# Keys ordered by token mod 8, fixed PSUM tiles and a spread inverse in a two-layer hybrid encoder

## The chip, the core and the metric

The kernel runs on one core of one Trainium2 chip. The core has five engines that work side by side, each from a queue of its own in order: TensorE (PE in the profile, with its weight loads as PEld), VectorE (DVE), ScalarE (ACT), GpSimd (POOL) and SyncE (SP), which here issues the DMA transfers. Data lives in HBM, in the on-chip SBUF (128 partitions) and in PSUM, into which TensorE writes its products. The metric is the time of one execution on the device in microseconds; shorter is better.

## The reference

One sequence of 1024 tokens of width 1024, float32, goes through two layers. Each layer has a token mixer and a squared-ReLU MLP, both between RMS norms.

```python
# layer 0, mixer A (8 heads of 64): three branches, merged by softmax-denominator weights
for window, dil in ((128, 1), (512, 4), (2048, 16)):
    radius = window // 2 // dil                     # 64 keys on each side in every branch
    split = lambda t: t.reshape(nB, H, S // dil, dil, hd).transpose(0, 1, 3, 2, 4)
    o, lse = banded_attention(split(q), split(k), split(v), bias, radius, radius)
o = sum(softmax(lse over branches) * o)             # and mixer B: banded GQA with a sink
# layer 1, mixer: one scan per direction, 16 heads of 64
sa = einsum('bhvk,bhk->bhv', state, -kk_t)
state = state * w_t + sa * (kk_t * a_t) + v_t * k_t
out_t = einsum('bhvk,bhk->bhv', state, r_t)
```

The attention's scores get a relative-position bias. With 1024 tokens, the third branch (dilation 16) is computed here in classes of tokens mod 8, with a bias that masks every second key.

## The kernel before

**Stages in order of time.** The v projection and bias tables (to 100 us), dilated attention A (100 to 455), banded attention B (to 547), the output projection (to 675), the MLP of layer 0 (to 1380), the projections of layer 1 (to about 1953), the chunked recurrence (its loop runs from 2077 to 2860), the output projection of layer 1 and its MLP. The change touches attention A (with the helpers that B also uses) and the recurrence.

**Who orders the work.** The program is written in order, and a planner then simulates it and lays down each engine's queue: among the instructions that are ready in its simulated time, the one that was written earliest goes first. Instructions inside the recurrence's units are written under `tc.high_priority(50)` (L1374), so they go ahead of other work. DMA issues stand in SP's queue, and a transfer that waits there holds up those behind it. Two engines that touch the same tile wait for each other by semaphores.

**Attention A.** Four pairs of heads, one after the other (L618). For each pair, v is loaded from DRAM in three layouts, one per branch: `v1` (11 blocks of 128 tokens in natural order, 3 loads), `v2` (classes mod 4, 2 loads) and `v3` (classes mod 8, 1 load). `make_q` (L536) and `make_k` (L548) project the pair's heads by PE in halves of 512 tokens and copy the results out of PSUM by ACT and DVE in turn: q as one tile whose two row halves hold a high and a low part, k as two tiles, high and low. The tokens stand in natural order in both. For each head and branch, `banded` (L566) goes through 8 tiles of 128 queries: two score products (L575, L576), the sum with the bias and the row minimum by DVE (L578), the exponential by ACT (L583), one or two transposes by PE (L587), a copy by ACT (L588), and one or two products with v (L592). Branch 1 reads the queries and 256 keys as runs. Branch 2 picks its 128 queries and 256 keys by a step of 4 tokens, branch 3 its 128 queries and 128 keys by a step of 8, both with

```python
def every(x, r, n, step):
    return x[:, r:r + (n - 1) * step + 1:step]
```

The bias of a head and branch is loaded from a table in DRAM (L645 to L648). `normalise` (L597) divides four tiles at a time. At the end of the pair the outputs of branches 2 and 3 (o2, o3) go to DRAM and come back in natural order as n2, n3 (L656 to L663); DVE and POOL merge them with o1 (L665 to L687).

**The recurrence.** Tokens go in chunks of 64; a step G handles two chunks of both directions and four heads, four steps are a batch, and eight batches make the 16 heads. Per step, `scan` (L1367) handles 8 units: 2 chunks x 2 head pairs x 2 directions, so four chains (`ci`) run interleaved, each with its own PSUM tile `ch` (tag c0 to c3, allocated anew for every unit) and its state `h`. A unit is: the state scaled by ACT (L1384); sums of two products (L1386, L1390), whose two halves stand in the same 64 columns on different rows; their copy to `y`, one half by ACT (L1392) and one by DVE (L1393); a product with the inverse (L1395), copied to `sv` by DVE and ACT (L1397, L1398); the new state's sum (L1401), which DVE scales and adds in two operations of 64x64 (L1407 for a first unit, L1410); the output products (L1416, L1421), written to the same columns as the state's sum; and their copy by ACT (L1424). After each unit `side()` (L1531) writes a piece of other work: `prep` of a step that lies eight ahead, `post` of the next step, `finish` of the last one.

`invert` (L1286) makes the inverses for a whole batch: two loads (L1290), 30 rounds of two DVE operations on all heads (L1295, L1297), then stores and loads through DRAM (L1302 to L1315). It is written as one piece at the second step of the batch before (L1513 to L1517); what follows it, up to the first half of the loads, is stepped by `first` (L1481) through `side()`, behind `post` of the next step. `post` of the next batch's first step, written at the fourth step, reads its results.

Of the kernel before, what the change touches and what calls it, by code (L numbers as in the profile page):

```python
# [15 lines left out]
P = 128  # L16
# [9 lines left out]
def fsl(i, n):  # L26
    return slice(i * n, (i + 1) * n)
# [444 lines left out]
def attention(tc, g, ap, ocd):  # L472
    nc = tc.nc
    with ExitStack() as es:
# [73 lines left out]
        def make_k(widx):  # L548
# [3 lines left out]
            for half, ps in project(widx):  # L552
                hs = fsl(half, 512)
                for j in range(2):
                    a, b = fsl(j, HD), fsl(1 - j, HD)
                    nc.scalar.activation(ks[j][a, hs], ps[a], AF.Copy)
                    nc.vector.tensor_tensor(out=kl[j][a, hs], in0=ps[a], in1=ks[j][a, hs], op=ALU.subtract)
                    nc.scalar.activation(ks[j][b, hs], ps[a], AF.Copy)
                    nc.vector.tensor_tensor(out=kl[j][b, hs], in0=ps[a], in1=ks[j][a, hs], op=ALU.subtract)
# [6 lines left out]
        def banded(tiles, q, k, bias, vtile, vcols, mneg, sink=None, W=256):  # L566
# [3 lines left out]
            for i, (qsl, ksl, blocks, boff) in enumerate(tiles):  # L570
# [4 lines left out]
                nc.tensor.matmul(ps[:, :n], lhsT=every(q, *qsl), rhs=every(kh, *ksl), start=True, stop=False)  # L575
                nc.tensor.matmul(ps[:, :n], lhsT=every(q, *qsl), rhs=every(kl, *ksl), start=False, stop=True)  # L576
# [32 lines left out]
        t1 = []  # L609
        for tt in range(TT):  # L610
            k0 = min(max(0, P * tt - 64), T - 256)
            bl = (7, 8) if tt == 0 else (9, 10) if tt == TT - 1 else (tt - 1, tt)
            t1.append(((P * tt, P, 1), (k0, 256, 1), bl, k0 - P * tt + P))
        t2 = [((512 * hf + r, P, 4), (r, 256, 4), (2 * r, 2 * r + 1), P * (1 - hf)) for hf in range(2) for r in range(4)]

        t3 = [((r, P, 8), (r, P, 8), (r,), 0) for r in range(8)]

        for pr in range(4):  # L618
            v1 = vp.tile([P, 11, 130], F32, tag="v1", name="v1")
            v2 = vp.tile([P, 8, 130], F32, tag="v2", name="v2")  # L620
            v3 = vp.tile([P, 8, 130], F32, tag="v3", name="v3")
            vc = vd[:, fsl(pr, P)]
            for v in (v1, v2, v3):
# [3 lines left out]
            blocks = lambda x: x.rearrange("(i p) c -> p i c", p=P)  # L627
            nc.sync.dma_start(out=v1[:, 0:7, cc], in_=blocks(vc[64:960, :]))
            nc.sync.dma_start(out=v1[:, 7:9, cc], in_=blocks(vc[0:256, :]))
            nc.sync.dma_start(out=v1[:, 9:11, cc], in_=blocks(vc[768:1024, :]))  # L630
            v4 = vc.rearrange("(j r) c -> j r c", r=4)
# [181 lines left out]
RC = 64  # L813
# [885 lines left out]
```

## Time and profile before

| | |
|---|---|
| median of 3 runs | 3665.36 us (3656.43 to 3675.8) |
| the profiled execution | 3664.62 us, its span 3662.9 us |
| granted PE clock over the span | 0.91 of full speed |
| attention A (100 to 455 us) | PE 339, DVE 184, ACT 198, POOL 26 us busy |
| the recurrence's loop (2077 to 2860 us) | PE 620, DVE 603, ACT 467, POOL 288 us busy, clock 0.80 |

A row of a group of instructions reads: line, engine, operation, output <- inputs, shapes, count | busy us, mean ns of one | idle time of its engine before them, and what ended it. A row of a stretch reads: its bounds and length, the busy time of each engine with the number of instructions, the granted clock of PE, the DMA engines' share and GB/s. A row of the waits reads: who waited <- for whom: us in total, times, the longest. A row of the timeline reads: start, length, engine, line, operation.

### The profile page before, as it was taken

The numbers are of one execution on the slowest core, as the hardware profiler recorded it, in microseconds if no ns is written. First come the engines' busy times: TensorE is split into PE (matmuls) and PEld (weight loads), VectorE is DVE, ScalarE is ACT, GpSimd is POOL, SyncE is SP. The second block draws the span as 40 slices with busy tenths as digits, with TensorE's granted clock in tenths as the row PEclk, the third lists the DMA queues.
The fourth block names the chain that finished last, engine by engine and source line by source line (L and its number), as shares of the span: only waits on it lengthen the run. The fifth ranks groups of instructions, "written<-read, shape, count | busy, mean of one in ns | idle before, by whom it ended". The sixth has DMA issues, their size and how long they took to land. (4 is left out here: it accounts for less than half of the span.)

```text
span 3662.9 us, 61199 instructions
## 1 busy us (share of the span) xinstructions
PE 3175.4 (87%) x22168; PEld 2587.1 (71%) x22168; DVE 2529.6 (69%) x4649; ACT 1849.7 (50%) x4244; POOL 1768.2 (48%) x1610
## 2 busy tenths in 40 slices
PE   7999998899999888888887687788777889999988
PEld 6788887688777676665566566666665768877766
DVE  3355564744499978977855778887776474449996
ACT  2366564455543347754433365555666445554333
POOL 1000001465598884455566344444431156558887
PEclk9999998899999998999896687778887899999999
DMA  6222214232231133257765354445444423323113
GB/s 202 72 80 81 72 55 171 76 138 108 70 139 37 79 113 107 95 185 232 228 221 155 94 127 107 106 127 122 121 100 133 129 84 135 115 71 131 42 74 115
DMA packets 408204, 425.70 MB, mean 116 GB/s; under 512 B 138155, under 2 KB 321579, under 8 KB 401756
## 3 DMA queue, kind: packets, MB, share of 16 engines
q1 hardware_dynamic: 406716, 417.58, 36.3%
q0 software_dynamic: 1184, 4.20, 0.4%
q8 instruction: 174, 2.85, 0.3%
q14 instruction: 130, 1.06, 0.1%
HBM read 290.83 MB, written 138.20 MB: 117 GB/s over the span
## 5 line engine op out<-in xcount | busy, mean ns | idle before, releaser
L101 PE MATMUL pm<-bhi,lo 128*128 128x512 f32 x840 | 331.8, 398 | 49.5 <-DVE lo L130 49.3
L130 DVE TENSOR_TENSOR lo<-x,hi 128x512 fp32r<-128x512 f32 x300 | 323.3, 1084 | 62.4 <-ACT hi L129 62.0
L129 ACT ACTIVATE hi<-x 128x512 fp32r<-128x512 f32 x300 | 189.1, 631 | 334.1 <-PE pm L100 129.1
L100 PE MATMUL pm<-blo,hi 128*128 128x512 f32 x840 | 330.2, 393 | 7.7 <-POOL blo L130 7.3
L99 PE MATMUL pm<-bhi,hi 128*128 128x512 f32 x840 | 319.2, 393 | 7.1 <-ACT bhi L129 6.7
L127 POOL TENSOR_TENSOR x<-w1r 128x512 f32<-128x512 f32 x160 | 214.6, 1345 | 203.1 <-DVE lo L130 178.3
L130 POOL TENSOR_TENSOR blo<-bx,bhi 128x512 fp32r<-128x512 f32 x138 | 221.1, 1603 | 30.5 <-ACT bhi L129 29.7
L1268 POOL TENSOR_TENSOR af<-af,amask 128x512 f32<-128x512 f32 x128 | 164.8, 1293 | 147.2 <-ACT af L1267 109.3
L101 PEld LDWEIGHTS pm<-bhi,lo 128*128 128x128 f32 x840 | 157.6, 188 | 101.9 <-DVE lo L130 70.8
L1264 PE MATMUL A<-zr,bk 128*128 128x128 f32 x1024 | 189.5, 349 | 44.3 <-DVE bk L1257 38.2
L905 POOL TENSOR_TENSOR wl<-wr,wh 128x512 fp32r<-128x512 f32 (+2 forms) x144 | 162.0, 1136 | 126.3 <-ACT wh L904 94.8
L127 POOL TENSOR_TENSOR bx<-w 128x512 f32<-128x512 f32 x140 | 215.1, 1539 | 9.5
L1264 PEld LDWEIGHTS A<-zr,bk 128*128 128x128 f32 x1024 | 168.1, 252 | 57.2 <-POOL bk L1258 22.0
L127 DVE TENSOR_TENSOR x<-h 128x512 f32<-128x512 f32 x140 | 195.6, 1409 | 5.3 <-ACT h L268 2.7
L100 PEld LDWEIGHTS pm<-blo,hi 128*128 128x128 f32 x840 | 158.4, 189 | 47.7 <-POOL blo L130 14.5
L99 PEld LDWEIGHTS pm<-bhi,hi 128*128 128x128 f32 x840 | 158.4, 189 | 40.0 <-ACT bhi L129 7.6
L99 PE MATMUL mm<-xmh,wh 128*128 128x512 f32 x384 | 163.0, 443 | 10.1 <-ACT wh L904 4.7
L1416 PE MATMUL c<-af,sv 128*64 128x64 f32 x1024 | 96.8, 273 | 74.7 <-DVE h L1410 67.7
L1410 DVE SCALAR_TENSOR_TENSOR h<-c,pc,hd 64x64 f32<-64x64 f32 x448 | 127.0, 284 | 49.6 <-PE c L1401 28.7
L583 ACT ACTIVATE S<-S,mneg 128x256 f32<-128x256 f32 (+2 forms) x256 | 124.7, 499 | 69.1 <-DVE mneg L578 46.2
L335 DVE TENSOR_TENSOR acc<-acc,pm 128x512 f32<-128x512 f32 x256 | 158.1, 675 | 0.3 <-PE pm L101 0.3
L886 DVE SCALAR_TENSOR_TENSOR x<-u,mu,x 128x512 f32<-128x512 f32 x192 | 153.4, 832 | 7.0 <-ACT x L884 4.3
(369 smaller groups left out, 9933.0 us busy)
## 6 DMA issues: line engine op xcount, KB each, us to landing
w1r<-in_mlp_w_dram SPq DMA_DIRECT2D x32, 1024.0 KB, 5.5
w<-in_mlp_w_dram SPq DMA_DIRECT2D x32, 1024.0 KB, 6.7
x<-x SPq DMA_DIRECT2D x64, 386.0 KB, 3.3
hd<-h SPq DMA_DIRECT2D x24, 1024.0 KB, 4.2
h<-hd SPq DMA_DIRECT2D x24, 1024.0 KB, 8.2
wr<-in_w_rkv_dram SPq DMA_DIRECT2D x96, 256.0 KB, 2.8
x<-xo SPq DMA_DIRECT2D x32, 512.0 KB, 3.7
rk<-rk SPq DMA_DIRECT2D x64, 256.0 KB, 3.7
```

The source lines that it names most:

```text
L99: nc.tensor.matmul(out, lhsT=ahi, rhs=bhi, start=start, stop=False)
L100: nc.tensor.matmul(out, lhsT=ahi, rhs=blo, start=False, stop=False)
L101: nc.tensor.matmul(out, lhsT=alo, rhs=bhi, start=False, stop=stop)
L127: add.tensor_tensor(out=y, in0=x, in1=blocks[term[2]], op=ALU.add if term[1] == "+" else ALU.subtract)
L129: nc.scalar.activation(hi, x, AF.Copy)
L130: sub.tensor_tensor(out=lo, in0=x, in1=hi, op=ALU.subtract)
L335: dve.tensor_tensor(out=a, in0=a, in1=banks[j], op=ALU.add if sign == "+" else ALU.subtract)
L886: nc.vector.scalar_tensor_tensor(out=x, in0=at(2 * i), scalar=mu[:, i, c, kt:kt + 1], in1=x, op0=ALU.mult, op1=ALU.add)
L905: nc.gpsimd.tensor_tensor(out=wlo, in0=wr, in1=whi, op=ALU.subtract)
L1264: nc.tensor.matmul(ps[:, fsl(u, P)], lhsT=bk[:, u, j].rearrange("p a b -> p (a b)"), rhs=zr[:, u].rearrange("p a b -> p (a b)"), start=Tru ...
L1268: nc.gpsimd.tensor_tensor(out=o, in0=o, in1=consts["amask"].unsqueeze(1).to_broadcast([P, 4, P]), op=ALU.mult)
L1410: nc.vector.scalar_tensor_tensor(out=hn[rows, cols], in0=ch[rows, 128:192], scalar=pc[rows, u:u + 1], in1=hd[rows, cols], op0=ALU.mult, op ...
```

## The change

**Attention.** `make_k` can write k in an order by token mod 8 (class r, then a = token // 8), by writing with a step of 128 elements. q is projected as before, and POOL copies it to `q8` in the same order. The key part of a tile is now a function of the k tile: branch 1 takes 8 runs of 32 keys, branch 2 two runs of 128, branch 3 one run of 128; queries of branches 2 and 3 are runs of `q8`. A tile of branch 2 now has the queries of one class mod 8 in place of 128 consecutive ones mod 4. `v1` becomes 16 blocks, two per query tile in the order of the keys, with 16 loads; `v2` is gone and branch 2 uses `v3`. The biases of branches 1 and 2 are loaded in natural order and put in the order of the keys by POOL (3 and 2 copies a head). n2 and n3 use the buffers of o2 and o3.

**The recurrence.** The four PSUM tiles are allocated once and set to zero. The two halves of the first sum stand in columns of their own, so that the tile's first 128 columns hold a block matrix with zeros elsewhere; one ACT copy of 128x128 makes `y`, and DVE's copy is gone. The state's sum has columns 256 to 383 in the same way, and one DVE operation of 128x128 makes the new state.

**The inverse.** It is begun at the batch's first unit (the loads), continued by two rounds (of two DVE operations) after each of units 4 to 18, and what follows, up to the first half of the loads, is written after unit 20 of 32.

```diff
+        def make_k(widx, perm=False):
...
+                kh_, kl_ = ([x.rearrange("p (r a) -> p a r", r=8)[:, fsl(half, 64)] if perm else x[:, fsl(half, 512)]
+                             for x in y] for y in (ks, kl))
+                if perm:
+                    ps = runs(ps, 8)
                 for j in range(2):
                     a, b = fsl(j, HD), fsl(1 - j, HD)
-                    nc.scalar.activation(ks[j][a, hs], ps[a], AF.Copy)
+                    nc.scalar.activation(kh_[j][a], ps[a], AF.Copy)
...
-                nc.tensor.matmul(ps[:, :n], lhsT=every(q, *qsl), rhs=every(kh, *ksl), start=True, stop=False)
+                nc.tensor.matmul(ps[:, :n], lhsT=every(q, *qsl), rhs=ksl(kh), start=True, stop=False)
...
-        t2 = [((512 * hf + r, P, 4), (r, 256, 4), (2 * r, 2 * r + 1), P * (1 - hf)) for hf in range(2) for r in range(4)]
-        t3 = [((r, P, 8), (r, P, 8), (r,), 0) for r in range(8)]
+        by8 = lambda x: x.rearrange("p (r a) -> p r a", r=8)
+        k0s = [min(max(0, P * tt - 64), T - 256) for tt in range(TT)]
+        t1 = [((P * tt, P, 1), lambda x, a=k0 // 8: by8(x)[:, :, a:a + 32], (2 * tt, 2 * tt + 1), 256 * (0 if tt == 0 else 2 if tt == TT - 1 else 1))
+              for tt, k0 in enumerate(k0s)]
+        t2 = [((r * P, P, 1), lambda x, r=r % 4: by8(x)[:, r:r + 5:4], (r % 4, r % 4 + 4), 256 * (r // 4)) for r in range(8)]
+        t3 = [((r * P, P, 1), lambda x, r=r: x[:, fsl(r, P)], (r,), 0) for r in range(8)]
...
+            for tt, k0 in enumerate(k0s):
+                win = vc[k0:k0 + 256, :].rearrange("(a i r) c -> i r a c", i=2, r=4)
+                for i in range(2):
+                    nc.sync.dma_start(out=v1[:, 2 * tt + i, cc], in_=win[i])
...
+            q8 = [qp.tile([P, T], F32R, tag=f"qp{j}", name=f"qp{j}", bufs=1) for j in range(2)]
+                    nc.gpsimd.tensor_copy(q8[j].rearrange("p (r a) -> p a r", r=8)[:, fsl(hf, 64)], runs(qs[j][:, fsl(hf, 512)], 8))
...
+                for i, f in enumerate((128, 64, 0)):
+                    nc.gpsimd.tensor_copy(b1[:, fsl(i, 256)].rearrange("p (r a) -> p r a", r=8), runs(nat[:, f:f + 256], 8).transpose([0, 2, 1]))
...
+                for i, f in enumerate((1, 0)):
+                    nc.gpsimd.tensor_copy(b2[:, fsl(i, 256)].rearrange("p (r a) -> p r a", r=2), runs(nat[:, f:f + 256], 2).transpose([0, 2, 1]))
...
-            n2 = op.tile([P, TT, 130], F32, tag="n2", name="n2")
+            n2 = op.tile([P, TT, 130], F32, tag="o2", name="n2")
...
+        chs = [psC.tile([P, 512], F32, name=f"c{d}") for d in range(4)]
+        for x in chs:
+            nc.vector.memset(x, 0.0)
...
-                            ch = psC.tile([P, 512], F32, tag=f"c{ci}", name=f"c{ci}")
+                            ch = chs[ci]
...
-                                nc.tensor.matmul(ch[fsl(1 - j, 64), 0:64], lhsT=af[:, j, 0:64], rhs=sv[:, j, :],
+                                nc.tensor.matmul(ch[rs[j], fsl(j, 64)], lhsT=af[:, j, 0:64], rhs=sv[:, j, :],
...
-                            nc.scalar.activation(y[0:64, 1], ch[0:64, 0:64], AF.Copy)
-                            nc.vector.tensor_copy(y[64:128, 0], ch[64:128, 0:64])
+                            nc.scalar.activation(y.rearrange("p j t -> p (j t)"), ch[:, 0:P], AF.Copy)
...
-                                        nc.vector.scalar_tensor_tensor(out=hn[rows, cols], in0=ch[rows, 128:192],
-                                                                       scalar=pc[rows, u:u + 1], in1=hd[rows, cols],
-                                                                       op0=ALU.mult, op1=ALU.add)
+                                    nc.vector.scalar_tensor_tensor(out=hn, in0=ch[:, 256:384], scalar=pc[:, u:u + 1], in1=hd,
+                                                                   op0=ALU.mult, op1=ALU.add)
...
-            if i == 1 and b + 1 < NB:
+            if i == 0 and b + 1 < NB:
                 bn = bs[b + 1]
                 bn.gi = invert(bn)
-                while not hasattr(bn, "inv"):
-                    next(bn.gi)
...
-            if i == 1 and b + 1 < NB:
-                b2.add(first(bn))
...
+                at = 8 * i + n[0]
+                if b + 1 < NB and (at == 1 or 4 <= at <= 18):
+                    next(bn.gi)
+                if at == 20 and b + 1 < NB:
+                    for _ in first(bn):
+                        pass
```

More of the change, by code (lines that the diff above doesn't have):

```diff
@@ L546, in make_q, with runs @@
             return qs
-        def make_k(widx):
+        def runs(x, n):
+            return x.rearrange("p (a r) -> p a r", r=n)
+        def make_k(widx, perm=False):
             ks = [qp.tile([P, T], F32R, tag=f"k{j}", name=f"k{j}") for j in range(2)]
@@ L655, in attention @@
                     nc.vector.tensor_tensor(out=o[:, :, 128 + j], in0=dall, in1=mneg, op=ALU.subtract)
-            o2v = o2d[pr].rearrange("(hf p r) c -> p hf r c", hf=2, r=4)
-            for hf in range(2):
-                nc.sync.dma_start(out=o2v[:, hf], in_=o2[:, fsl(hf, 4), :])
-            nc.sync.dma_start(out=o3d[pr].rearrange("(j r) c -> j r c", r=8), in_=o3)
-            n2 = op.tile([P, TT, 130], F32, tag="n2", name="n2")
-            n3 = op.tile([P, TT, 130], F32, tag="n3", name="n3")
+            for d, o in ((o2d, o2), (o3d, o3)):
+                nc.sync.dma_start(out=d[pr].rearrange("(j r) c -> j r c", r=8), in_=o)
+            n2 = op.tile([P, TT, 130], F32, tag="o2", name="n2")
+            n3 = op.tile([P, TT, 130], F32, tag="o3", name="n3")
             nc.sync.dma_start(out=n2, in_=o2d[pr].rearrange("(t p) c -> p t c", p=P))
@@ L1189, in rwkv_scan @@
         hbd = [[t1.tile([P, P], F32, name=f"h{d}{i}") for i in range(2)] for d in range(4)]
-        ybd = [t1.tile([P, 2, RC], F32, name=f"y{d}") for d in range(4)]
-        for x in sum(hbd, ybd):
+        yst = [t1.tile([P, 2, RC], F32, name=f"y{d}") for d in range(4)]
+        for x in sum(hbd, []):
             nc.gpsimd.memset(x, 0.0)
+        chs = [psC.tile([P, 512], F32, name=f"c{d}") for d in range(4)]
+        for x in chs:
+            nc.vector.memset(x, 0.0)
         bk = t1.tile([P, 4, 2, 2, RC], F32, name="bk")
@@ L1384, in scan @@
                                 nc.scalar.activation(hd, h, AF.Copy, scale=pc[:, u:u + 1])
+                            rs = [fsl(1 - j, 64) for j in range(2)]
                             for j in range(2):
[L1386 removed]
+                                nc.tensor.matmul(ch[rs[j], fsl(j, 64)], lhsT=af[:, j, 0:64], rhs=sv[:, j, :],
                                                  start=True, stop=h is None)
@@ L1403, in scan @@
                                 hn = hbd[ci][c]
-                                for j in range(2):
-                                    rows = cols = fsl(j, 64)
-                                    if h is None:
-                                        nc.vector.tensor_scalar(out=hn[rows, cols], in0=ch[rows, 128:192],
-                                                                scalar1=pc[rows, u:u + 1], scalar2=None, op0=ALU.mult)
-                                    else:
-                                        nc.vector.scalar_tensor_tensor(out=hn[rows, cols], in0=ch[rows, 128:192],
-                                                                       scalar=pc[rows, u:u + 1], in1=hd[rows, cols],
-                                                                       op0=ALU.mult, op1=ALU.add)
+                                if h is None:
+                                    nc.vector.tensor_scalar(out=hn, in0=ch[:, 256:384], scalar1=pc[:, u:u + 1], scalar2=None,
+                                                            op0=ALU.mult)
+                                else:
+                                    nc.vector.scalar_tensor_tensor(out=hn, in0=ch[:, 256:384], scalar=pc[:, u:u + 1], in1=hd,
+                                                                   op0=ALU.mult, op1=ALU.add)
```

64 lines of the change are left out of this document (27 added, 37 removed).

## The prediction

> **What bounds the kernel now.** The page comes first, for the span and the engines; then the stretches of the two stages that the change touches (attention's dilated part, 100 to 455 us, and the recurrence, 2077 to 2860 us), with three single batches of the recurrence below them.
>
> ```profile
> span 3662.9 us, 61199 instructions
> ...
> PE 3175.4 (87%) x22168; PEld 2587.1 (71%) x22168; DVE 2529.6 (69%) x4649; ACT 1849.7 (50%) x4244; POOL 1768.2 (48%) x1610
> ```
> ```profile
> core 0: us, PE busy (x) PEld busy (x) DVE busy (x) ACT busy (x) POOL busy (x), PEclk, DMA share, GB/s
> 100.00:455.00 355.00, 338.54 (x1945) 305.88 (x1946) 184.14 (x689) 197.96 (x503) 25.61 (x41) 0.94 0.25 76
> ...
> 2077.00:2860.00 783.00, 619.96 (x10094) 503.80 (x10092) 603.35 (x1728) 467.06 (x1568) 288.35 (x358) 0.80 0.45 116
> ```
> ```profile
> 2508.00:2618.00 110.00, 85.61 (x1381) 69.01 (x1379) 85.72 (x237) 65.04 (x218) 48.01 (x60) 0.83 0.48 117
> ...
> 2711.00:2786.00 75.00, 55.71 (x1020) 43.06 (x1020) 58.84 (x204) 45.66 (x163) 10.65 (x16) 0.78 0.41 112
> 2786.00:2860.00 74.00, 58.20 (x1112) 44.65 (x1112) 44.71 (x144) 48.45 (x163) 8.29 (x11) 0.79 0.40 120
> ```
>
> Attention is TensorE's: PE is busy for 338.5 of 355 us, ACT for 198, DVE for 184, POOL for 26. What shortens PE's queue shortens this stage. The recurrence is nobody's: PE 620, DVE 603, ACT 467 of 783 us, all of them waiting in turn. It has 256 units (32 steps x 2 chunks x 4 chains), 783/256 = 3.06 us each, and the waits show the ring in which a unit goes round:
>
> ```profile
> ACT sv L1398 <- DVE sv L1397: 78.3, 93, 3.7
> ...
> PE c L1416 <- DVE h L1410: 67.7, 78, 4.4
> ...
> PE c L1395 <- DVE y L1393: 37.3, 41, 5.0
> ...
> DVE y L1393 <- ACT y L1392: 28.0, 28, 9.1
> ```
>
> The columns are us in total, times and the longest. The fourth row matters: L1392 and L1393 read different rows and write different parts of y, yet DVE's half begins only when ACT's is done. [...]
>
> **Part 1, attention.** Removed are strided reads by PE. The windows of one head's three branches, run back to back with no projection between, show the price (start, length, engine, line; L575 is the first score product, L592 the first product with v that follows the two score products):
>
> ```profile
> 347.97 0.19 PEld L575 LDWEIGHTS s<-k,q 128*128 128x128 f32 x1
> ...
> 348.33 0.56 PE L592 MATMUL o<-v,ST 128*128 128x65 f32 x4
> ...
> 350.07 0.31 PEld L575 LDWEIGHTS s<-k,q 128*128 128x128 f32 x1
> ...
> 350.73 0.57 PE L592 MATMUL o<-v,ST 128*128 128x65 f32 x4
> ...
> 351.26 0.31 PEld L575 LDWEIGHTS s<-k,q 128*128 128x128 f32 x1
> ...
> 358.77 0.32 PEld L575 LDWEIGHTS s<-k,q 128*128 128x128 f32 x1
> ...
> 359.32 0.59 PE L592 MATMUL o<-v,ST 128*128 128x65 f32 x4
> ```
>
> From first load to the next kind of product a tile of branch 1 (step 1) takes 348.33 - 347.97 = 0.36 us, of branch 2 (step 4) 0.66 us, of branch 3 (step 8, half as many keys) 0.55 us. After the change all three read runs: branch 1 eight runs of 32 keys, branch 2 two of 128, queries and branch 3 one. I price them all at 0.36 us. Each branch has 8 tiles x 8 heads = 64: branch 2 saves 64 x 0.30 = 19.2 us, branch 3 64 x 0.19 = 12.2 us, together 31.4 us of PE's queue.
>
> Is something else just behind PE? The groups of this stage and, for the copies, of the recurrence:
>
> ```profile
> L583 ACT ACTIVATE S<-S,mneg 128x256 f32<-128x256 f32 x129 | 63.5, 506 | 36.4 <-DVE mneg L578 33.7 <-DVE mneg L581 1.0 <-DVE rec L603 0.4
> ...
> L578 DVE CUSTOM_DVE_ANT_0 S<-s,b 128x256 f32<-128x256 f32 x128 | 52.1, 420 | 30.3 <-PE s L576 19.2 <-PE pt L587 6.5 <-ACT ST L588 1.4
> ...
> L588 ACT ACTIVATE ST<-pt 128x256 f32<-128x256 f32 x129 | 47.3, 378 | 30.8 <-PE pt L587 22.8 <-PE o L592 6.2
> ...
> L578 DVE CUSTOM_DVE_ANT_0 S<-s,b 128x128 f32<-128x128 f32 x64 | 18.4, 291 | 31.9 <-PE s L576 15.4 <-PE pt L587 12.4 <-ACT ST L588 2.9
> ...
> L588 ACT ACTIVATE ST<-pt 128x128 f32<-128x128 f32 x64 | 16.2, 272 | 13.3 <-PE pt L587 12.7
> ...
> L557 DVE TENSOR_TENSOR kl<-mm,k 64x512 fp32r<-64x512 f32 x20 | 13.7, 687 | 10.1 <-ACT k L556 9.9
> ...
> L556 ACT ACTIVATE k<-mm 64x512 fp32r<-64x512 f32 x20 | 11.7, 590 | 6.8 <-DVE kl L559 4.2 <-PE mm L101 2.2 <-PE s L575 0.3
> ```
> ```profile
> L1410 DVE SCALAR_TENSOR_TENSOR h<-c,pc,hd 64x64 f32<-64x64 f32 x448 | 127.0, 284 | 49.6 <-PE c L1401 28.7 <-ACT y L1392 4.2 <-PE c L1390 2.6
> ...
> L1393 DVE COPY y<-c 64x64 f32<-64x64 f32 x256 | 54.8, 226 | 31.3 <-ACT y L1392 28.0
> ...
> L1392 ACT ACTIVATE y<-c 64x64 f32<-64x64 f32 x256 | 51.9, 211 | 26.1 <-PE c L1390 22.1 <-PE c L1386 1.7
> ...
> L1339 ACT ACTIVATE sv<-B 64x512 f32<-64x512 f32 x62 | 36.5, 589 | 1.5 <-PE B L1336 0.4 <-PE c L1416 0.2
> ...
> L1305 ACT ACTIVATE xbt<-nb 64x512 f32<-64x512 f32 x14 | 15.2, 1084 | 3.1 <-DVE nb L1297 1.8 <-DMA xd<-xbt 1.1
> ...
> L1331 POOL COPY vr<-v 128x256 f32<-128x256 f32 x31 | 13.5, 436 | 70.0 <-PE B L1336 40.2 <-issue 13.6 <-PE c L1401 13.5
> ```
>
> ACT needs 0.506 + 0.378 = 0.88 us for a tile of 256 keys. Branch 2 now starts a tile every 351.26 - 350.07 = 1.19 us; minus 0.30 is 0.89 us, just at ACT's pace, so the gain is taken almost whole but no more could be. Over the stage ACT has 157 us free, enough.
>
> Added work: (a) The two copies and two subtractions per head half that build the permuted k write with a step of 128 elements: 32 on ACT and 32 on DVE over the four pairs. No row has that write. From below it costs nothing; from above it is what a transposed read costs ACT, 1084 against 589 ns for the same 64x512 (L1305, L1339): +0.5 us for each of 64, 32 us on two engines. The cover is PE's queue of projections; it is missing once, before the first tile of the first pair, where 4 + 4 such operations stand between the last product and the first score: I take 8 x 0.5 = +4 us.
> [...]
> (b) POOL copies: 16 of 128x512 for the permuted q, 24 + 16 of 128x256 for the biases. At 436 ns for 128x256 (L1331) that is 40 x 0.44 + 16 x 0.87 = 31 us on an engine that is idle for 329 of 355 us: 0. Without cover, behind a late q copy, five bias copies of a head cost 2.2 us, four pairs 9 us.
> (c) SP issues 16 loads of v a pair in place of 5, and no second v:
>
> ```profile
> 356.60 0.37 SPq L628 DMA_DIRECT2D v<-vd  x1
> ```
>
> 16 x 0.37 = 6 us of issuing. v1's buffer comes free after branch 1 of the pair's second head, as now, and branch 2 alone then runs 8 x 0.89 = 7 us before branch 3 and the next pair: 0. Behind them wait the bias loads of the next head, which have two buffers. (d) The merged buffers of o2 and n2, o3 and n3: their next writer comes after the writer of o1, which is released last: 0.
> Attention: -31.4 + 4 = -27.4 us; ends -31.4 (all covered) and +9.6 (32 + 9 exposed).
>
> **Part 2, a unit of the recurrence.** Copying y: ACT's 211 ns and then DVE's 226 ns become one ACT copy of 128x128, 272 ns by L588: 0.226 + 0.211 - 0.272 = 0.165 us less on the ring, and no hand-over. Writing h: two operations of 284 ns become one of 128x128. L578 goes from 291 to 420 ns for 128 more elements, about 1 ns each, so 284 + 64 = 350 ns; 0.218 us less on the ring, 224 times. PE has the same products. The tile that is no longer allocated anew costs a memset: 0. DVE loses 224 x 0.218 + 54.8 = 103.6 of its 603 us, ACT gains 256 x 0.061 = 15.6 us.
> What reaches the time? At most the ring's whole 256 x 0.165 + 224 x 0.218 = 91 us (or DVE's 104). At least what PE visibly waits for: 78 x 0.218 + 41 x 0.165 = 24 us. DVE is busy for the same 78% of the batches at 2508 and 2711 though they last 110 and 75 us, which speaks for the high end; the last batch has 14.1 us less DVE than the one before it and is only 1 us shorter, which speaks for the low. I take the middle, -58 us.
>
> **Part 3, the inverse spread.** It is moved, not made cheaper: one batch's 60 DVE operations, then its loads and stores.
>
> ```profile
> 2509.00:2618.00 109.00, 25.18 (x60) 2.14 (x2) 0.16 (x1) 0.83 0.47 115
> ...
> 2711.00:2786.00 75.00, 20.90 (x60) 2.17 (x2) 0.17 (x1) 0.78 0.41 112
> ```
> ```profile
> 2713.49 6.44 DMA nb<-nd
> 2774.32 6.44 DMA xd<-xbt
> ...
> 2784.45 2.37 DMA xt<-xd
> ```
>
> The first fence is busy time of tile nb, the second the chain that ended last. In the batch from 2711 us the inverse starts loading at once and stores at 2774, after 63 of 75 us: the planner already spreads it over most of a batch, since the scan's instructions go first. The text now ends it after 20 of 32 units, which is 47 of 75 us there and 69 of 110 us in a long batch. So the words promise more than the queue changes: I take 0. Ends: the stretches that the late end costs, at most the 12.5 us from 2774.32 to 2786.82 in each of 7 batches on one side (-87 us, though only the last batches show it), and the same on the other.
>
> **Sum.** The profiled execution took 3664.62 us, 1.7 us around its span and 0.7 us under the median 3665.36: 3664.6 - 27.4 - 58 = 3579 us.
>
> **The rivals.**
> 1. The ring is the time: everything cut shows. -104 and -31.4: 3529 us. For it the steady 78%; against it the last batch. Chance 0.15.
> 2. Attention gives nothing, because the stepped k writes (32 us) stand in ACT's and DVE's queues ahead of what PE needs, and the recurrence only gives the 24 us of visible waits: 3641 us. For it DVE's and ACT's alternation in L556 and L557, where each waits for the other; against it 16 us of idle PE in all. Chance 0.13.
> 3. With sums in columns of their own, the output product (L1416) no longer waits for h at all: its 67.7 us go, and y's 42 us by 58/91, 27 us: 3664.6 - 27.4 - 67.7 - 27 = 3542 us. [...] Chance 0.07. [...]
> 4. Slower: the inverse ends too late. Its last pieces are now issued behind units 17 to 20, while the next batch's first correction needs it by unit 26. From the last step on 12.5 us of stores and loads follow, four units; the point is therefore unit 22. If each of the 15 pieces slips behind a unit's boosted DVE work by some 1.5 us, the end slips by 23 us, less the 6 us (two units) of slack: 17 us in each of 7 batches, +119: 3698 us. Against it the gap that DVE has in every batch. Chance 0.06.
>
> **How the numbers follow.** Forecast 0.59, rivals 0.15, 0.13, 0.07, 0.06. Half a per cent is 18 us, about what the three runs of before spread (3656.43 to 3675.8) and what a measurement can tell. Faster: 0.59 + 0.15 + 0.07 and 0.05 of rival 2, 0.86. Same: the rest of rival 2, 0.08. Slower: 0.06. The range goes from rival 1 to rival 2, 3525 to 3642 us.
>
> **What would show it.** Attention's stretch falls from 355 to about 328 us, L575 and L576 load in 0.19 us in every branch, and the steps of 0.66 and 0.55 us become 0.36. If the permuted k writes stay at 590 and 690 ns, the +4 was wrong; if they show some 1.1 us and PE has new gaps, rival 2. In the recurrence DVE falls to about 500 us, h is one operation of 350 ns, y one ACT copy of 272 ns, and the stretch is near 725 us. If L1416 still waits for h, rival 3 is out; if the first group of each batch waits for xt, rival 4 is in. A forecast of 3579 is wrong as a whole if attention does not shrink or the recurrence shrinks by less than 24 us.

## The result, and the profile after

The changed kernel takes 3611.59 us (median of 4 runs, 3604.49 to 3616.05), beside 3664.94 us for the kernel before in the same sitting: a ratio of 0.9851, interval 0.9820 to 0.9882. The forecast was 3579 us with a range of 3525 to 3642. So it is 1.5% faster, inside the range, and gains 33 us less than the forecast. The profiled execution took 3609.13 us, 55.5 us less than that of before. In a later sitting one execution of the kernel before took 4388.38 us; it was a slow one and counts in no ratio and no median here.

The page after, span and engines:

```profile
span 3607.4 us, 61062 instructions
...
PE 3133.2 (87%) x22168; PEld 2552.3 (71%) x22168; DVE 2440.2 (68%) x4157; ACT 1855.4 (51%) x4244; POOL 1813.2 (50%) x1654
```

The two stretches, attention's dilated part and the recurrence's loop (columns as in the prediction's second fence):

```profile
101.00:445.00 344.00, 317.99 (x1937) 279.74 (x1938) 188.88 (x681) 201.55 (x497) 58.79 (x75) 0.92 0.24 70
...
2062.00:2804.00 742.00, 591.66 (x10095) 491.64 (x10094) 505.04 (x1233) 469.26 (x1572) 285.49 (x359) 0.82 0.48 123
```

Nearly all of the gain lies there. The attention mixers end at 533.6 us in place of 545.9 (12.3 us; attention B, which the change touches only by a slice written in another way, is 3 us shorter too). The loop, from its first product to the last copy of its output, takes 741.8 us in place of 783.4 (41.6 us). The other 1.6 us are between and behind them. Forecast were 27.4 and 58.

The groups of attention after, by form. L582 is the first score product (L575 before), L563 and L564 are k's copy and subtraction (L556, L557), L642 the copy of q, L654 and L660 those of the biases:

```profile
L583 PEld LDWEIGHTS s<-kl,qp 128*128 128x128 f32 x128 | 26.6, 207 | 0.1
...
L642 POOL CAST qp<-q 128x512 fp32r<-128x512 f32 x16 | 16.8, 1105 | 94.3 <-DVE q L544 43.0 <-ACT ST L595 25.6 <-PE s L583 13.4
...
L654 POOL COPY b<-bn 128x256 f32<-128x256 f32 x18 | 11.6, 688 | 61.3 <-DVE mneg L585 61.3
...
L660 POOL COPY b<-bn 128x256 f32<-128x256 f32 x12 | 4.6, 415 | 39.2 <-DVE mneg L585 39.2
```

The same for L563 and L564 from 101 to 330 us, where every one of them is stepped (after 330 us each has four more for attention B, which write runs and take 584 and 686 ns):

```profile
L563 ACT ACTIVATE k<-mm 64x512 fp32r<-64x512 f32 x16 | 17.0, 1088 | 6.0 <-DVE kl L566 3.4 <-PE mm L101 2.3
...
L564 DVE TENSOR_TENSOR kl<-mm,k 64x512 fp32r<-64x512 f32 x16 | 17.0, 1063 | 12.1 <-ACT k L563 12.0
```

And a tile of branch 3, from its first load to the next kind of product:

```profile
408.69 0.19 PEld L582 LDWEIGHTS s<-k,qp 128*128 128x128 f32 x1
...
408.97 0.53 PE L599 MATMUL o<-v,ST 128*128 128x65 f32 x3
```

The loads with a step (0.31 us before) now take 0.21 us on the mean, and 0.19 us where PE has its full clock, as here; the tile of branch 3 takes 0.28 us in place of 0.55. The stepped k writes went from 590 and 687 ns to 1088 and 1063 ns.

The groups of the loop after. L1424 is h (L1410 before), L1410 is y (L1392 and L1393), L1412 and L1428 are the products that wait for them (L1395, L1416); below them the waits of the loop:

```profile
L1428 PE MATMUL c<-af,sv 128*64 128x64 f32 x1024 | 94.5, 270 | 88.0 <-DVE h L1424 77.7 <-ACT sv L1414 5.4 <-DVE h L1421 4.0
...
L1424 DVE SCALAR_TENSOR_TENSOR h<-c,pc,hd 128x128 f32<-128x128 f32 x224 | 74.3, 348 | 63.4 <-PE c L1417 40.4 <-PE c L1412 6.3 <-PE c L1408 4.6
L1410 ACT ACTIVATE y<-c 128x128 f32<-128x128 f32 x256 | 66.0, 269 | 30.7 <-PE c L1408 27.3 <-PE c L1404 1.5
```
```profile
PE c L1428 <- DVE h L1424: 77.7, 55, 4.3
ACT sv L1414 <- DVE sv L1413: 74.2, 63, 3.9
...
DVE h L1424 <- PE c L1417: 40.4, 33, 6.9
...
PE c L1412 <- ACT y L1410: 4.6, 9, 1.4
```

Both operations cost what was forecast (348 ns against 350, 269 against 272), and PE's wait for y fell from 37.3 to 4.6 us. Its wait for h did not fall in this kernel: 77.7 us, against 67.7 before. DVE's busy time fell by 98 us (603.35 to 505.04) and the loop by 42.

### The profile page after: what moved, and what is told of

It is laid out like the page before. It is cut to its first block, busy times and chain, and to the rows that moved or that the text cites. A ratio compares the mean times of both kernels' runs of the same rounds, so it can differ in the third digit from the quotient of the medians.

```text
span 3607.4 us, 61062 instructions
## 1 busy us (share of the span) xinstructions
PE 3133.2 (87%) x22168; PEld 2552.3 (71%) x22168; DVE 2440.2 (68%) x4157; ACT 1855.4 (51%) x4244; POOL 1813.2 (50%) x1654
## 5 line engine op out<-in xcount | busy, mean ns | idle before, releaser
L1428 PE MATMUL c<-af,sv 128*64 128x64 f32 x1024 | 94.5, 270 | 88.0 <-DVE h L1424 77.7
L100 PE MATMUL mm<-xml,wh 128*128 128x512 f32 x384 | 156.0, 406 | 0.0
L1273 DVE TENSOR_TENSOR bk<-x,ipr 64x256 f32<-64x256 f32 x128 | 114.0, 891 | 61.8 <-PE A L1292 57.1
## 6 DMA issues: line engine op xcount, KB each, us to landing
x<-xo SPq DMA_DIRECT2D x32, 512.0 KB
```

The source lines that it names most:

```text
L100: nc.tensor.matmul(out, lhsT=ahi, rhs=blo, start=False, stop=False)
L1273: nc.vector.tensor_tensor(out=quad(bk[rows, :, j, j]), in0=kd[rows], in1=quad(ipr[rows]), op=ALU.mult)
```

## The experiments

Two theories stood at the start. **Sizes**: the parts do together what they do alone, and the missing 33 us are the stepped k writes and a ring term taken too high. **Parts in each other's way**: each part gives its share alone, but something is lost when they stand together. Every kernel below computes the whole reference. The table has all of them; "attention's end" is the end of the last product of attention B, "loop" the recurrence's loop as above, both from the profiled execution. The kernel before ran again in each sitting (medians 3664.94 to 3668.62 us), and each ratio goes by its own sitting.

| kernel | median us | ratio and interval | attention's end | loop |
|---|---|---|---|---|
| before | 3664.94 | 1 | 545.9 | 783.4 |
| the change | 3611.59 | 0.9851 (0.9820 to 0.9882) | 533.6 | 741.8 |
| attention alone | 3677.39 | 1.0031 (1.0019 to 1.0043) | 535.1 | 810.6 |
| PSUM tiles alone | 3604.80 | 0.9830 (0.9813 to 0.9847) | 543.8 | 719.9 |
| inverse alone | 3656.83 | 0.9970 (0.9959 to 0.9980) | 547.1 | 774.9 |
| the change, k copies writing runs | 3599.60 | 0.9820 (0.9801 to 0.9839) | 515.4 | 737.9 |
| the change without the inverse | 3573.26 | 0.9733 (0.9712 to 0.9754) | 533.3 | 708.3 |
| the same, k copies writing runs | 3559.08 | 0.9699 (0.9678 to 0.9719) | 515.7 | 706.0 |
| the same, output products first | 3546.36 | 0.9666 (0.9646 to 0.9687) | 512.0 | 686.5 |
| the change without attention's part | 3590.30 | 0.9783 (0.9765 to 0.9800) | 544.9 | 715.4 |
| the change, h zeroed by DVE | 3584.79 | 0.9785 (0.9770 to 0.9800) | 531.9 | 716.5 |
| the change, PSUM zeroed thrice | 3613.03 | 0.9858 (0.9844 to 0.9871) | 536.4 | 739.1 |
| without the inverse, zeroed thrice | 3569.91 | 0.9752 (0.9732 to 0.9772) | 522.0 | 701.7 |
| output products first, zeroed thrice | 3545.04 | 0.9675 (0.9661 to 0.9690) | 510.6 | 690.9 |

### Attention's part alone

The first four hunks of the diff on the kernel before: `make_k`, `banded`, the tiles and loads of attention A, the slice of attention B.

```diff
-            ks = make_k(4 + pr)
+            ks = make_k(4 + pr, True)
...
-                q, k = qs[j], ks[j]
+                k = ks[j]
```

> The attention part alone on the kernel before. Theory: the parts stand in different stretches and add up; this one gives what the stretch up to the end of attention B lost between the two traces, 545.9 - 533.6 = 12 us, so 3653 us, with the recurrence's loop at its old 783 us. Rival: what the stage gave was lost again only together with the other parts, and alone it gives the 27 us of the forecast, 3638 us.

Measured: 3677.39 us, 0.3% slower than before. Attention ends 10.8 us earlier, and the recurrence, whose text this kernel does not touch, takes 27 us longer. The profiled execution was the longest of this kernel's, 3693.6 us, so part of the 27 may be that execution; but outside attention and the loop, too, it was 12.6 us longer than the kernel before, which is most of the 16 us that it lies above its median. Its loop:

```profile
2076.00:2887.00 811.00, 639.67 (x10095) 518.94 (x10095) 615.93 (x1728) 465.12 (x1570) 290.87 (x359) 0.77 0.44 112
```

DVE has the same 1728 instructions as before and is busy for 615.93 us in place of 603.35. What differs is their order. From 1900 us on, the longest series of instructions that stands in the same order in both kernels (by their tiles, others left out between them) takes in 1961 of DVE's 2482 instructions and 10627 of PE's 13939. The likely reason, argued from how the planner works: it goes through the whole program in its simulated time; an edit in attention can shift that time, and which instructions are ready first later on then comes out another way. That an unchanged stage moves by more than the change in the changed one was in neither theory.

### The PSUM tiles alone

```diff
-                            ch = psC.tile([P, 512], F32, tag=f"c{ci}", name=f"c{ci}")
+                            ch = chs[ci]
...
-                            nc.scalar.activation(y[0:64, 1], ch[0:64, 0:64], AF.Copy)
-                            nc.vector.tensor_copy(y[64:128, 0], ch[64:128, 0:64])
+                            nc.scalar.activation(y.rearrange("p j t -> p (j t)"), ch[:, 0:P], AF.Copy)
```

> The recurrence's fixed PSUM tiles alone (one copy of y, one operation for h), the inverse as before. Theory: the shorter ring gives the whole of the 42 us by which the loop fell (783 to 742 us), so 3623 us. Rival: the inverse's new places give most of it; then this one gives under 20 us, 3645 us or more.

```profile
2071.00:2791.00 720.00, 581.12 (x10095) 482.63 (x10095) 493.77 (x1233) 469.86 (x1572) 287.50 (x359) 0.84 0.50 128
```

Measured: 3604.80 us. The loop is 63.5 us shorter, where the forecast's term was 58, and this part alone already gives more than the whole change.

### The spread inverse alone

```diff
-            if i == 1 and b + 1 < NB:
+            if i == 0 and b + 1 < NB:
                 bn = bs[b + 1]
                 bn.gi = invert(bn)
-                while not hasattr(bn, "inv"):
-                    next(bn.gi)
```

> The spread inverse alone. Theory: the planner spread it before, so 0 us, within 8 us of 3665. Rival: it gives most of the loop's 42 us, 3630 us or less. Second rival: it ends too late for the next batch and alone it costs time, 3680 us or more.

Measured: 3656.83 us, 0.3% faster, the loop 8.5 us shorter. By their ratios the three parts alone sum to +0.31 - 1.70 - 0.30 = -1.69%, near the -1.49% of the change; but that the sum comes out is a coincidence, as the runs with two of the three parts show.

### Runs in the k copies

What the k copies write becomes runs of 64 elements, and what they read from PSUM is picked with a step of 8; the order of the keys is the same.

```diff
-                kh_, kl_ = ([x.rearrange("p (r a) -> p a r", r=8)[:, fsl(half, 64)] if perm else x[:, fsl(half, 512)]
+                kh_, kl_ = ([x.rearrange("p (r a) -> p r a", r=8)[:, :, fsl(half, 64)] if perm else x[:, fsl(half, 512)]
...
-                    ps = runs(ps, 8)
+                    ps = ps.rearrange("p (a r) -> p r a", r=8)
```

> The changed kernel, with k's copies turned round: they read PSUM with a step of 8 elements and write runs of 64, in place of reading runs of 8 and writing with a step of 128. Theory: the step costs on the SBUF side alone, so the copies fall from 0.98 to about 0.6 us on ACT and from 0.99 to 0.69 us on DVE (22 us of both together), and attention gets 5 us shorter: 3606 us. Rival: a step costs on either side, the copies stay at 0.98 us or above and the time at 3611 us.

Its two stretches, and its k copies:

```profile
101.00:427.00 326.00, 304.05 (x1941) 267.75 (x1942) 178.17 (x683) 186.78 (x498) 57.91 (x75) 0.96 0.25 74
2047.00:2785.00 738.00, 589.93 (x10094) 491.63 (x10094) 503.50 (x1233) 468.58 (x1572) 284.75 (x358) 0.82 0.48 124
```
```profile
L564 DVE TENSOR_TENSOR kl<-mm,k 64x512 fp32r<-64x512 f32 x20 | 13.7, 687 | 7.9 <-ACT k L563 7.7
...
L563 ACT ACTIVATE k<-mm 64x512 fp32r<-64x512 f32 x20 | 11.4, 588 | 4.8 <-PE mm L101 2.3 <-DVE kl L566 2.3
```

Reading PSUM with a step of 8 cost nothing in these copies of 64x512 (588 and 687 ns, against 590 and 687 before the change); writing SBUF with a step had cost 0.50 us on ACT and, with k read by the same step, 0.38 us on DVE. (The 0.98 and 0.99 us of the expectation are means that hold attention B's copies without a step.) Attention ends at 515.4 us, 30.5 us earlier than before and 18 us earlier than in the change, where 5 had been expected. Of the 30.5 us, 27.6 are attention A's (its last product with v ends at 426.5 us in place of 454.1) and the rest B's. In A, from 101 us to that product, PE is busy for 303.6 us in place of 337.6 and idle for 22.0 in place of 15.5. Not all of the 34 us need be the shorter loads, since the granted clock is 0.96 in place of 0.94. Part of the new idle time is a longer wait for DVE's row minima, first before the change, then in this kernel:

```profile
PE s L575 <- DVE mneg L578: 2.1, 5, 1.1
```
```profile
PE s L582 <- DVE mneg L585: 9.5, 11, 3.5
```

From the change's 344.0 us to 326.0 there are 18 us: PE's idle time goes from 26.0 to 22.0 us, and its busy time from 318.0 to 304.1, at a granted clock of 0.96 in place of 0.92. The kernel as a whole gains 0.31% by the ratios, 11 us; the two intervals overlap, but that of a repeat of the change's order in a later sitting (0.9844 to 0.9871, below) lies clear of this one. The loop is as in the change, and so is the order of the later queues: all of DVE's, ACT's and POOL's instructions behind attention stand in the same order. So an edit in attention does not always lay the later queues anew.

### Without the spread inverse, with both forms of the k copies

```diff
-            if i == 0 and b + 1 < NB:
+            if i == 1 and b + 1 < NB:
                 bn = bs[b + 1]
                 bn.gi = invert(bn)
+                while not hasattr(bn, "inv"):
+                    next(bn.gi)
```

> The changed kernel without the spread inverse alone (k's copies still write with a step). Theory A (spread takes back some 20 us): loop about 720 us, attention's end stays at 533 us, time 3590 us. Rival B (the order of the later queues, not the spread): loop about 740 us or longer, time 3610 us or more.

> The changed kernel without the spread inverse, and with k's copies writing runs. Theory A, the spread inverse takes back some 20 us of the short ring and attention's gain is carried to the end: attention ends at about 515 us (as in the run with runs in the k copies), the recurrence's loop is about 720 us long (as in the run with the PSUM part alone), and the time is 3664.6 - 30.5 - 63.5 = about 3571 us. Rival B, the loop is longer because attention changed the order of all later queues: the loop stays at about 740 us, the time at 3590 to 3600 us. Rival C, the loop grows as it did with attention alone (+27 us): some 3600 us or more.

The loop without the inverse, first with stepped writes, then with runs:

```profile
2062.00:2771.00 709.00, 582.04 (x10095) 483.31 (x10096) 490.41 (x1232) 472.25 (x1572) 288.06 (x359) 0.85 0.51 129
```
```profile
2047.00:2753.00 706.00, 581.52 (x10094) 483.23 (x10094) 493.33 (x1232) 471.04 (x1571) 288.42 (x358) 0.84 0.51 129
```

Measured: 3573.26 and 3559.08 us, both better than either theory had them, with loops of 708.3 and 706.0 us. Beside attention's part and the PSUM tiles, then, the loop is 33 us longer with the spread inverse than without it. The first expectation put this down to the inverse and the short ring; the next run refutes that.

### The change without attention's part

The hunks of the recurrence, inverse and all, on the kernel before.

```diff
-            for x in sum(hbd, ybd):
+            for x in sum(hbd, []):
...
-            if i == 1 and b + 1 < NB:
+            if i == 0 and b + 1 < NB:
```

> The recurrence's part with the spread inverse, attention as before. Theory A (the spread costs some 20 us where the ring is short): loop about 740 us, time about 3625 us. Rival B (the spread is worth -8 us here too, and the loop of the changed kernel is longer because attention moved the later queues): loop about 710 us, time 3596 us.

```profile
2071.00:2787.00 716.00, 592.63 (x10095) 487.50 (x10096) 486.90 (x1232) 468.90 (x1572) 289.38 (x359) 0.84 0.50 128
```

Measured: 3590.30 us, loop 715.4. Here the inverse beside the PSUM tiles takes 4.5 us off the loop. So the 33 us are seen only where all three parts stand together. Attention's part and the inverse share no tile and no stretch of time; what they share is the planner's run.

### Two neutral edits

To tell order from interaction, the change itself got edits that do next to nothing: the eight state tiles zeroed by DVE in place of POOL, and the four PSUM tiles zeroed three times.

```diff
         for x in sum(hbd, []):
-            nc.gpsimd.memset(x, 0.0)
+            nc.vector.memset(x, 0.0)
```

> The changed kernel with one neutral edit: the eight state tiles of 128x128 are zeroed once by DVE in place of POOL, long before the loop, about 1 us of work. It lays the later queues in another order (about a quarter of the rows of PE's queue stand elsewhere). Theory order: the length of the recurrence's loop is set by the order that the planner happened to lay, so it moves from 742 us to anywhere between 705 and 750 us, and the time moves with it, 3575 to 3620 us. Rival interaction: the spread inverse really costs 30 us beside this attention; the loop stays at 735 to 748 us, the time at 3605 to 3618 us.

```diff
-        for x in chs:
+        for x in chs * 3:
             nc.vector.memset(x, 0.0)
```

> The changed kernel with another neutral edit: the four PSUM tiles are set to zero three times in place of once, eight more operations of 485 ns at 1935 us, 3.9 us of DVE at most. Theory order: the loop moves away from 742 us by 10 us or more, here or in the other neutral edit, with no relation to the 3.9 us. Rival interaction: the loop stays at 735 to 748 us.

> The changed kernel without the spread inverse, with the four PSUM tiles set to zero three times. Without this edit its loop took 708 us. Theory order: the loop is longer now, 715 to 740 us, or in any case not tied to whether the inverse is spread. Rival interaction: it stays at 703 to 714 us, and about 30 us below the changed kernel under the same edit.

The loops, in the order of the expectations:

```profile
2064.00:2780.00 716.00, 588.23 (x10093) 489.62 (x10092) 494.06 (x1232) 467.07 (x1569) 287.81 (x358) 0.83 0.49 127
```
```profile
2065.00:2805.00 740.00, 590.56 (x10099) 492.55 (x10096) 503.00 (x1233) 469.57 (x1573) 284.76 (x359) 0.82 0.48 124
```
```profile
2054.00:2756.00 702.00, 578.74 (x10094) 479.92 (x10094) 489.88 (x1232) 471.78 (x1571) 288.79 (x358) 0.85 0.51 130
```

Zeroing h by DVE took 25 us off the loop (741.8 to 716.5) and, by the ratios, 0.66% or 24 us off the time (3584.79 us), with all three parts in place. It ran in one sitting with the second neutral edit, whose median is 3613.03 us. The longest series in the same order as in the change takes in 1640 of DVE's 1988 instructions from 1900 us on. The second edit turned out not to lay another order at all: apart from the added operations, DVE's, ACT's and POOL's instructions stand exactly as in the change, against what its expectation assumed, and so they do in the third kernel beside the one without the inverse. So those two runs test neither theory (the third kernel's 701.7 us also lies below both of its ranges); they are repeats of an order: 739.1 after 741.8 and 737.9, 701.7 after 706.0 and 708.3. Over the repeats of an order the loop kept within 7 us. An order that differs through nothing but the engine of eight early memsets moved it by 25. The kernel without the inverse was measured in one order alone, so how much of the 33 us is the inverse and how much the order stays open.

Over the whole loop the difference shows in what PE waits for. With h zeroed by DVE:

```profile
PE c L1428 <- DVE h L1424: 55.0, 47, 4.3
```

In the change this wait is 77.7 us, and 79.4 and 77.7 us in the two other kernels that have its order; all of PE's idle time in the loop falls from 150.3 to 127.8 us.

How two orders part is seen in DVE's own timeline, some 30 us into the loop. First the change, then the same with h zeroed by DVE (start, length, engine, line, operation):

```profile
2093.32 0.87 DVE L1424 SCALAR_TENSOR_TENSOR h<-c,pc,hd 128x128 f32<-128x128 f32 x3
2095.13 0.23 DVE L1413 COPY sv<-c 64x64 f32<-64x64 f32 x1 [0.94 <-PE c L1412]
2100.02 1.67 DVE L1461 SCALAR_TENSOR_TENSOR ot<-ot,par,osq 128x256 f32<-128x256 f32 x2 [4.66 <-ACT osq L1458]
2101.61 0.95 DVE L1463 SCALAR_TENSOR_TENSOR gt<-ot,par,gt 128x256 f32<-128x256 f32 x1
2102.48 0.86 DVE L1273 TENSOR_TENSOR bk<-x,ipr 64x256 f32<-64x256 f32 x2
```
```profile
2094.96 0.87 DVE L1424 SCALAR_TENSOR_TENSOR h<-c,pc,hd 128x128 f32<-128x128 f32 x3
2095.74 0.72 DVE L1273 TENSOR_TENSOR bk<-x,ipr 64x256 f32<-64x256 f32 x1
2096.77 0.23 DVE L1413 COPY sv<-c 64x64 f32<-64x64 f32 x1 [0.30 <-PE c L1412]
2098.80 1.47 DVE L1461 SCALAR_TENSOR_TENSOR ot<-ot,par,osq 128x256 f32<-128x256 f32 x2 [1.80 <-ACT osq L1458]
```

In the change, the two `ot` operations of a step already scanned stand in DVE's queue ahead of the `bk` operations, and DVE stands still for 4.66 us until ACT has their input. In the other order one `bk` operation has gone ahead, and the same wait is 1.80 us. This is one place, shown for how such a difference looks; the 25 us are not traced place by place.

This also puts a price on the attention stage. The repeat without the inverse ran attention's queues in the same order as the change and yet finished the stretch in 332 us. The stretch and thirteen microseconds inside it, then the same thirteen in the change:

```profile
101.00:433.00 332.00, 304.09 (x1936) 265.41 (x1937) 187.95 (x681) 200.31 (x497) 58.78 (x75) 0.97 0.24 73
255.00:268.00 13.00, 13.00 (x122) 12.94 (x120) 9.48 (x52) 11.19 (x36) 3.98 (x6) 1.00 0.09 23
```
```profile
255.00:268.00 13.00, 12.63 (x66) 12.59 (x67) 5.49 (x32) 6.23 (x20) 0.77 (x2) 0.55 0.15 52
```

PE is busy for 13.00 and 12.63 of the 13 us, with 122 products in one and 66 in the other, at a clock of 1.00 and 0.55. Against the kernel with runs (304.1 us busy, 22.0 idle), the stepped writes cost 6 us of PE's idle time here (27.9), and the other 12 us of the change go with PE busy for longer, 318.0 us in place of 304.1, at a granted clock of 0.92 in place of 0.97. That execution was 8.8 us shorter than its kernel's median. Over attention A the granted clock was 0.94 or 0.95 in the four profiles with k copied as before the change, 0.92 or 0.93 in five of the six with stepped writes and 0.97 in this one, and 0.95 to 0.97 in the four that write runs. So a lower granted clock is the usual case beside the stepped writes, though not in every execution.

### The output products first

On the kernel without the inverse and with runs in the k copies, the four output products of a unit are written ahead of the operation that makes the new state, with which they share the PSUM tile.

```diff
+                            for j in range(2):
+                                nc.tensor.matmul(ch[fsl(j, 64), 128:192], lhsT=sv[:, j, :], rhs=af[:, j, 64:128],
+                                                 start=True, stop=h is None)
...
+                            if not last:
                                 hn = hbd[ci][c]
...
-                            for j in range(2):
-                                nc.tensor.matmul(ch[fsl(j, 64), 128:192], lhsT=sv[:, j, :], rhs=af[:, j, 64:128],
-                                                 start=True, stop=h is None)
```

> As the changed kernel without the spread inverse and with runs in the k copies, but in a unit of the recurrence the four output products are written ahead of the operation that makes the new state, so that PE no longer waits for that operation's read of the same PSUM tile. Theory ring: the new state is made after four more products, 0.68 us by PE's busy time for them in a unit (91.2 + 78.3 us over 256 units in the run with the PSUM part alone), and 224 units on the ring make the loop 100 to 150 us longer than without this edit. Rival queue: what counts is PE standing still in front of the output products, 47 + 4 us by the waits in that run; the loop gets up to 50 us shorter. Between: the other three chains fill the 0.68 us and nothing changes within 15 us.

> The kernel with the output products ahead of the new state (no spread inverse, runs in the k copies), with the four PSUM tiles set to zero three times. Without this edit its loop took 686 us, 20 us less than its own base (706 us). If writing the products first is a real gain, its loop is again some 20 us below that of the kernel without the spread inverse under the same edit; if that gain was only the order that the planner laid, the difference may be nothing or have the other sign. Time 3540 to 3570 us.

Waits of the loop without and with the edit:

```profile
PE c L1427 <- DVE h L1423: 57.2, 50, 4.9
```
```profile
ACT ot L1436 <- DVE h L1432: 65.4, 74, 2.6
...
PE c L1403 <- ACT ot L1436: 42.2, 52, 2.9
...
DVE h L1432 <- PE c L1424: 29.5, 25, 3.8
```

Measured: 3546.36 us and a loop of 686.5, the shortest of all; under the second zeroing 3545.04 and 690.9. PE's 57.2 us in front of the output products are gone. In their place ACT's copy of the output now waits for DVE to have read h from the same tile (65.4 us), and the next unit's first product waits for ACT (42.2). The ring did not grow by the 0.68 us that it was charged with; the loop is 11 to 20 us shorter (beside 701.7 and 706.0 us; the first of these two has stepped k copies, but the same order of the later queues). Since the later queues of the two runs with this edit stand in one order, they are one order measured twice, and 25 us is what an order alone can move: how much of the 11 to 20 us is the edit stays open.

## Why the prediction was right, and where it was wrong

The time lies in the range and both stages shrank as forecast, but neither by its term: up to attention's end 12.3 us in place of 27.4, in the loop 41.6 in place of 58.

**Attention's loads: right in each load, but not taken whole.** At the full clock a load takes the 0.19 us of the forecast. In the kernel with runs, which has no stepped write to pay for, attention A ends 27.6 us earlier, 4 us short of the 31.4. The step that failed here is "so the gain is taken almost whole": PE now waits more for the engines just behind it, 9.5 us for DVE's row minima (`mneg`) in place of 2.1 and 4.6 us for ACT's copy of the transposed exponentials (`ST`) in place of 2.3, and is idle for 22.0 us in place of 15.5. The sum had put this at nothing. PE's busy time fell by 34 us, but at a clock of 0.96 in place of 0.94, so the loads' part of it can't be told. That the 27.6 us lie beside the forecast's net of 27.4 is luck, since this kernel has no stepped write for the +4.

**"I take 8 x 0.5 = +4 us" for the stepped k writes: the price was right, the cover was not all that counts.** The step took its bound from above as the price of an operation and a cover for all but one pair. The price was at that bound on ACT (+0.50 us) and below it on DVE (+0.38), some 27 us in all in place of 32. PE's idle time grew by 4 to 6 us over that of the kernel with runs, as forecast. What the sum lacked is the other 12 to 14 us of the stretch's 18: PE busy for longer, at a granted clock of 0.92 in place of 0.96 or 0.97. The execution at 332 us shows that the writes don't always bring it, so the forecast's row for it would have been a range and not a price.

**POOL's copies and SP's issues at nothing: right.** The q copies cost 1105 ns and the first branch's bias copies 688, more than the 0.87 and 0.44 us taken from L1331: 16 x 1.105 + 24 x 0.688 + 16 x 0.415 = 41 us in place of 31. The kernel with runs pays them all and attention still ends 30.5 us earlier.

**The ring, -58: near by itself, and hidden by the order.** Alone it gives 63.5 us of loop; beside the inverse 59.5 (774.9 to 715.4), beside attention's part 102 (810.6 to 708.3). The last figure holds the long execution of attention's part alone, and all three compare kernels whose later queues stand in two orders, so each is good to some 25 us only. The 58 were the middle between 24 and 91 and came from no mechanism of their own, so that two of the three lie within 6 us of it is luck. Of the two waits that the low end counted, the one for y went (37.3 to 4.6 us) and the one for h did not (67.7 to 77.7 us in the change, 55.0 us with h zeroed by DVE).

**The inverse, 0: right within what can be told.** The 60 operations of a batch ended 13 to 55 us ahead of the batch's end before, and 35 to 68 us after (last operation on `nb` against the batch's last output copy); the spread moved the end by 22 us in the seventh batch (13 to 35) and by less in the others (38 to 39 in the third). Its effect on the loop is -8.5, -4.5, +33.5 and, with h zeroed by DVE in the change, +8 us against the kernel without it (708.3).

**The step that failed for the loop** is the one that isn't written: the working took the queues of every stage as given apart from the edits, and each term as its sum of durations. The front of this document says that a planner lays them. 41.6 us in place of 58 is one draw; the same three parts in another order give 66.9 us (783.4 - 716.5) and a time of 3585, 6 us from the forecast. That nearness is chance too: attention's end gave 14.0 us there in place of 27.4, and the loop 8.9 more than its 58.

**The rivals.** The first (3529 us, everything cut shows) falls with 98 us of DVE saved against 42 of loop. The second had the price of the writes nearly right (some 27 of its 32 us), and its new idle time of PE is there (26.0 us in place of 15.5), but its result is wrong: attention's end still moved by 12.3 us, and the recurrence gave more than 24. The third is out by its own test: L1428 waits for h for 77.7 us though its columns are its own. In the last experiment, too, ACT's copy of the output waits for 65.4 us until DVE has read other columns of the same tile. The fourth would have needed the inverse to end late; it ended earlier.

## What to carry to other kernels

Where a planner lays the queues, an edit in one stage can change the order of work in a later one: look first at which stages moved that the diff does not touch, and before a part is blamed or praised for some tens of microseconds, give the kernel a neutral edit, see that its order really differs, and take the spread as the error of a single comparison (here 25 us, 0.7%). If a reordering copy out of PSUM is needed, try the step on the PSUM side and write SBUF in runs (here 588 ns in place of 1088 for ACT's copy of 64x512). Removing a wait on a shared PSUM tile moved it here to the next engine that touches the tile (57.2 us of PE's waiting gone, 65.4 us of ACT's in their place), so ask which one that is and what stands behind it.

## What the runs showed of the hardware

Writing 64x512 into SBUF with a step of 128 elements took 1088 ns for ACT's copy and 1063 ns for DVE's subtraction (which also reads k with that step), against 588 and 687 with runs. The latter two read PSUM with a step of 8 and took no longer than the 590 and 687 ns of the kernel before, which reads it without one.

By the profile, PE was busy without a break in the change's attention for over 10 us and yet held at half clock. Three stretches, each 3.4 us long (the columns of the stretches again; the third figure from the end is the granted clock):

```profile
258.40:261.80 3.40, 3.40 (x18) 3.40 (x18) 1.12 (x6) 0.67 (x2) 0.00 (x0) 0.50 0.10 32
261.80:265.20 3.40, 3.40 (x19) 3.40 (x19) 0.75 (x6) 1.59 (x5) 0.00 (x0) 0.50 0.01 2
265.20:268.60 3.40, 3.40 (x20) 3.40 (x20) 1.65 (x10) 1.82 (x7) 0.56 (x1) 0.50 0.00 0
```

PE is busy for 3.40 of 3.40 us in all three, by the profile's modelled ends of matmuls, at a granted clock of 0.50; what the clock goes by was not tried. Whether the stepped writes provoke it is open too: five of the six profiles that have them show the lowest clocks (0.92 and 0.93), but the sixth shows 0.97, and half clock is in the kernel before as well (0.50 from 254.0 to 267.6 us, 0.94 over attention A).
